# Low parts of the weights on VectorE, and mean and running-sum products queued with a margin, in a float32 encoder layer on one core

## The chip, the cores and the metric

The kernel runs on one core of one Trainium2 chip. The metric is the device time of one execution in microseconds (us). The kernel before has three timed runs: 1586.59, 1587.16 and 1590.54 us, median 1587.16. Engines are named as in the profile: PE is TensorE's matrix products, PEld its weight loads, DVE is VectorE, ACT is ScalarE, POOL is GpSimd, SP is SyncE, on which this kernel issues all its DMAs.

## The reference

One layer of a streaming encoder is computed for 1056 tokens: 1024 of a new stream and 32 that continue a running stream with 512 cached keys and values. There are 1024 features, 8 heads of 64, 512 channels in the convolution branch and 4096 hidden units, all in float32. Cut to what matters:

```python
p = einsum('btd,de->bte', x, w_in)        # GLU a, b | q | k | v | forget logits | 2 x 1024 gates
u = a * sigmoid(b)                         # convolution branch
y = depthwise_conv(u, w_dw) + b_dw         # causal, width 31
y_conv = silu(layer_norm(y)) @ w_conv_out  # mean and variance over the 512 channels
logf = log_sigmoid(p_f + b_f); c = cumsum(logf)
s = q k / 8 + c_q - c_k                    # masked, softmax, times v -> o
m = sigmoid(g_conv) * y_conv + sigmoid(g_attn) * (o @ w_attn_out)
x1 = layer_norm(alpha * x + m @ w_o)
x2 = layer_norm(alpha * x1 + relu(x1 @ w_up)**2 @ w_down)
```

Outputs are x2 and the new convolution rows, keys, values and log forget values.

## The kernel before, in words

**Layout and number format.** Features lie on the 128 partitions and tokens along the free axis, in three chunks of 352. A float32 product is made as three products of a faster format: each operand is split into a high part and a low part, and high x high, high x low and low x high are added in PSUM. So every weight is split on the chip. It arrives by DMA in halves of 128x512 (`raw`), ACT copies the half into `whi` with rounding, and a subtraction `raw - whi` leaves `wlo`. `Weights.split` does this for 264 halves; the first two subtractions are on DVE, 262 on POOL.

**Stages.** (1) Projections: GLU tiles, values, queries and keys (four tiles each, `ps_q`, `ps_k`), and gate tiles 0 to 5 (`ps_g`). (2) Attention over 8 heads and the cached stream (`ps_s` are its scores), with gate tiles 6 to 15 as filler products. (3) The merge, `w_o` with the first layer norm (`_n` in the names), eight blocks of hidden units (`ps_up`, `ps_dn`), and a tail with the last layer norm.

**The convolution branch.** Beside stage 1 a generator `conv()` issues the depthwise convolution on DVE: four channel tiles `ca`, 30 multiply-adds each of 128x1086. Then come three column blocks c0, c1, c2 of 362 columns, one after the other. Each is a layer norm over the channels: `total` adds the four tiles to `lns_dve_m`; `norm_rows` multiplies it on PE with a constant matrix (`ps_mu_c`), subtracts the mean on DVE, squares on ACT, adds the squares to `lns_dve_vc`, multiplies again (`ps_var_c`) and takes root and reciprocal (`rstd_c`). Then `done` makes, tile by tile, a multiply-add on DVE, a sigmoid on ACT (`csig`), a second multiply-add on DVE, the high part on ACT (`csh`) and the low part (`csl`), and DMAs both parts to a scratch `s_s`. A second generator, `forget()`, makes the log forget values `logf` in a chain of small DVE operations and sums them over the tokens with two products (`ps_cum`) and a transpose (`ps_cumt`) on PE.

**What sets the order.** Every engine works in the order of issue. The class `Issue` keeps a model clock for each engine. A generator yields what its next step needs; `service`, called between groups of products, goes on with a generator when `due(need)`, the modelled time at which these operands stand ready, is not past the modelled time of PE. What is left of the generators when the gate tiles of stage 1 are through is issued by `I.flush()` whatever its due time, and only then do the loads of the first head and the attention follow. In the listings and the profile, L202 and L206 are the product and the transpose in `Issue`, L214 an ACT operation, L218, L223, L227, L231 and L235 copy, tensor_tensor, tensor_scalar, scalar_tensor_tensor and reciprocal, L197 a DMA. In the changed kernel each of these stands three lines lower.

Of the kernel before, what the change touches and what calls it, by code (L numbers as in the profile page):

```python
# [17 lines left out]
P = 128  # L18
# [37 lines left out]
WARM = 19  # L56
GB = 2
# [21 lines left out]
class Issue:  # L79
    """Issues instructions and keeps a rough clock for each engine. Every engine works in the order of  # L80
    issue, so work that stands ready is put in front of work that would wait: `fill` and `service`."""
# [32 lines left out]
    def due(self, need):  # L114
        if callable(need):
            return 0.0 if need() else 1e12
        if isinstance(need[0], str):
            return max(self.t[e] for e in need[:-1]) - need[-1]
        return max(max(self.ready(a), self.free.get(a.tensor.name, 0.0)) for a in need)
# [19 lines left out]
    def finish(self, last):  # L139
        """issues what is left of a background stream and of those before it in its group"""  # L140
# [11 lines left out]
    def drain(self):  # L152
        """issues all background streams: the oldest that can go on, or else the first that can"""
# [6 lines left out]
    def pick(self, n, bias=0.0):  # L160
        """the engine that would be through with a tensor_tensor first"""
        pool, dve = (max(self.t[e], self.t["pe"] - 500) for e in ("pool", "dve"))
        return "pool" if pool + n * 1.97 + 150 + bias < dve + n * 1.01 + 80 else "dve"
# [74 lines left out]
class Slots:  # L238
    """A tile pool whose slots the clock knows"""
# [24 lines left out]
def hybrid_layer(ctx: ExitStack, tc, io):  # L264
# [15 lines left out]
    # ---- scratch in DRAM  # L280
# [20 lines left out]
    # ---- weights: streamed, split in two float32r parts that add up to the float32 exactly  # L301
# [10 lines left out]
    class Weights:  # L312
        def __init__(self):
            self.raw, self.parts, self.taken, self.done, self.halves = [], [], 0, 0, 0

# [7 lines left out]
        def split(self):  # L323
# [8 lines left out]
            tt(lo, raw, f32(hi), SUB, "dve" if i < 2 else "pool")  # L332
# [26 lines left out]
    def mm3(ps, terms, late=False, low=False):  # L359
        """ps = sum of w.T x over terms; each float32 product as hi hi + hi lo + lo hi"""  # L360
# [17 lines left out]
    # ---- layer norm of one block of tokens, features on the partitions of several tiles: 1/std and  # L378
    # the centred rows in place; a background stream whose steps come when their operands stand ready
# [16 lines left out]
    def norm_rows(pl, psl, tiles, mean, tag, n, s, engs, done):  # L396
        yield [s]
# [9 lines left out]
        yield [s]  # L407
# [7 lines left out]
    # sixteen rows of tiles: the inputs, then what the merge reads, then the residual and hidden units  # L415
# [11 lines left out]
    def gates(tiles, banks, staging, tag, bufs, xh_read=None):  # L427
        """the gates before their sigmoid; xh_read is called with the last tile's products of xh through"""
# [27 lines left out]
    # =============================================================== projections, convolution  # L456
    with pool("conv") as pv_, pool("a") as pa, pool("pa", space=PSUM) as psa:
# [40 lines left out]
        # products of ones, read by nobody, bring the tensor engine to its full clock as the inputs arrive  # L498
# [61 lines left out]
        def conv():  # L560
# [7 lines left out]
            for c in range(3):  # L568
                cs = slice(c * CC, (c + 1) * CC)
                tiles = [ca[j][:, cs] for j in range(NJ)]  # L570
                s = total(pv_, tiles, f"m{c}", CC, ("dve", "dve", "pool", "pool"))

                def done(rstd, c=c, cs=cs, tiles=tiles):
                    for j, y in enumerate(tiles):
# [8 lines left out]
                        tt(lo[:, j, :], y, f32(hi[:, j, :]), SUB, "pool")  # L583
                    for dst, src in ((s_s[0], hi), (s_s[1], lo)):
# [3 lines left out]
                        else:  # L588
# [5 lines left out]
                                     ("dve", "dve", "pool", "pool"), done)  # L594

        # ---- log sigmoid of the forget logits and its running sums
        logf = pa.tile([P, 9, H], F32, name="logf")

        def forget():
# [21 lines left out]
            yield [logf, lfs]  # L621
# [10 lines left out]
            yield [cum]  # L632
# [8 lines left out]
        # the first tiles go chunk by chunk, as the inputs arrive  # L641
# [17 lines left out]
        # ---- values, tokens on partitions  # L659
        for half in range(2):  # L660
            ws = [W.take() for g in range(2)]
            for t in range(9):
# [15 lines left out]
                tt(vs[:r, :, DH:P], vv, f32(vs[:r, :, 0:DH]), SUB, "pool")  # L678
# [12 lines left out]
        # ---- queries (times -1/8) and keys, features on partitions  # L691
        for m in range(4):
            for name in "qk":
                w = W.take()
                for c in range(NCH):
# [7 lines left out]
                    tt(lo, a, f32(hi), SUB, "pool")  # L703
# [23 lines left out]
    # =============================================================== attention, branch gates  # L727
    with pool("b") as pb, pool("pb", space=PSUM) as psb:
# [21 lines left out]
        # the first products of the merge, as the rows of the inputs come free  # L750
# [28 lines left out]
        # operands of one head: [kh; kh] on [qh; ql] and [kl; c, 1] on [qh; 1, -c] add up to all of  # L779
        # -(q k / 8 + c_q - c_k)  # L780
# [17 lines left out]
        # two heads of the running stream: their cached keys and values are split on the chip  # L798
# [87 lines left out]
        class Rows:  # L886
            """128 query rows of one head against their keys"""
# [56 lines left out]
        class Stream:  # L944
            """the new queries of two heads of the running stream against cached and new keys"""
# [93 lines left out]
    # =============================================================== merge, output projection, FFN  # L1039
# [62 lines left out]
    def run_sum(cs, m, s, tag, eng="dve"):  # L1102
        """adds tile m of a block of tokens to the running sum over features"""
# [12 lines left out]
    def squares(sq, t, total, nth, n, tag):  # L1116
        """squares one more tile and adds the square before it to the running sum"""
# [15 lines left out]
    def norm_out(cs, tag, s, emit, need=()):  # L1133
        """layer norm of a block of tokens in place, a background stream as well"""
# [66 lines left out]
    with pool("h") as ph:  # L1201
# [28 lines left out]
        def down_first(wd, cs):  # L1230
            """the first tiles, with what the newest hidden units add put last"""
# [44 lines left out]
        def output(cs, new=False):  # L1276
            """where a block of tokens puts its results: in place, or two tiles at a time"""
# [21 lines left out]
        # the last tokens go through the last hidden units block by block, with the weights kept  # L1299
# [28 lines left out]
        # the last block: the mean over its first tile is taken off as soon as it is known, which leaves  # L1328
# [134 lines left out]
```

## Time and profile before

| what | before |
|---|---|
| median of three runs | 1587.16 us |
| profiled execution, first to last instruction | 1585.9 us |
| PE busy | 1506.2 us (95%), 9524 products |
| DVE busy | 911.8 us (57%), 1385 instructions |
| ACT busy | 487.4 us (31%), 1048 instructions |
| POOL busy | 655.2 us (41%), 557 instructions |
| mean granted TensorE clock | 0.979 |

The profile is of one execution, and its own time is the span of 1585.9 us; the lowest timed run is 0.7 us above it and the median 1.3 us. A share of busy time is a mean over all stages; which wait ends last is read stage by stage. In rows of the timeline the first two numbers are the start and the duration of one instruction in us; `x4` says that four alike stand in the row; brackets give the idle time of the engine before it and what released it. Rows of windows give for a stretch its length, the busy time and the instructions of PE, PEld, DVE, ACT and POOL in that order, the granted TensorE clock, the DMA share and GB/s.

### The profile page before, as it was taken

The page shows a single profiled execution, that of the slowest core. Times are in us where ns is not written, and L with a number is a line of the kernel's source. Part 1 is how long each engine was busy: PE and PEld are TensorE (multiplying, and loading weights), DVE is VectorE, ACT ScalarE, POOL GpSimd, SP SyncE. Part 2 cuts the span into 40 slices and gives each one's busy share as a digit, 9 for nine tenths or more (in the row PEclk, how much of TensorE's full clock was granted, in tenths as well). Part 3 has the DMA queues.
Part 4 walks back from the last instruction along what each step waited for, and adds up shares of the span by engine and source line. Part 5 has one row for each costly group of instructions (what it writes and reads, how often), then busy time and mean ns, then how long its engine had stood idle before and what let it go on. Part 6 is the DMA issues. An engine that isn't in the chain of part 4 may idle for free.

```text
span 1585.9 us, 24681 instructions
## 1 busy us (share of the span) xinstructions
PE 1506.2 (95%) x9524; PEld 1476.5 (93%) x9524; DVE 911.8 (57%) x1385; ACT 487.4 (31%) x1048; POOL 655.2 (41%) x557
## 2 busy tenths in 40 slices
PE   9999598699999999999899999999999999999985
PEld 8999598698989999899899999999999999999984
DVE  4799999653656654864887243333424333342588
ACT  4211211453656655433554121111111111111133
POOL 2436576633445533657765222222222222222346
PEclk9999699899999999999999999999999999999998
DMA  6214443437555557626531111111111111114412
GB/s 199 69 46 137 134 136 125 151 114 219 152 142 147 146 150 269 210 87 190 154 96 54 47 47 41 54 41 50 44 47 47 41 54 41 54 41 140 153 37 73
DMA packets 113731, 165.56 MB, mean 104 GB/s; under 512 B 19146, under 2 KB 71626, under 8 KB 113614
## 3 DMA queue, kind: packets, MB, share of 16 engines
q1 hardware_dynamic: 113614, 163.99, 33.6%
q8 instruction: 75, 1.23, 0.3%
q14 instruction: 42, 0.34, 0.1%
HBM read 120.38 MB, written 43.54 MB: 103 GB/s over the span
## 4 chain that ended last, share of the span: by engine, by line
PE 67%; DVE 7%; issue 2%; ACT 1%; DMA 1%; POOL 1%; SPq 0%; DVEq 0%; ACTq 0%; POOLq 0%
PE ps_dn L202 22%; PE ps_up L202 22%; PE ps_g L202 8%; PE ps_yc L202 3%; PE ps_o L202 2%; PE ps_s L202 2%; PE ps_pv L202 2%; PE ps_tr L206 2%; PE ps_yo L202 2%; DVE acc L231 2%; DVE lnvar_n L223 2%; DVE acc L223 0%; DVE yg L223 0%; DVE rstd_n L235 0%; DMA g_s<-gt 0%
## 5 line engine op out<-in xcount | busy, mean ns | idle before, releaser
L223 POOL TENSOR_TENSOR wlo<-raw,whi 128x512 fp32r<-128x512 f32 (+1 forms) x262 | 381.8, 1478 | 605.6 <-ACT whi L214 598.7
L214 ACT ACTIVATE whi<-raw 128x512 fp32r<-128x512 f32 (+1 forms) x264 | 151.9, 623 | 396.9 <-issue 337.6
L202 PE MATMUL ps_dn<-hh,whi 128*128 128x352 f32 x768 | 249.3, 325 | 0.0
L202 PE MATMUL ps_dn<-hl,whi 128*128 128x352 f32 x768 | 247.8, 323 | 0.8 <-DVE hl L223 0.8
L202 PE MATMUL ps_dn<-hh,wlo 128*128 128x352 f32 x768 | 248.0, 323 | 0.0
L223 DVE TENSOR_TENSOR acc<-ps_dn,acc 128x352 f32<-128x352 f32 x168 | 87.8, 523 | 194.5 <-PE ps_dn L202 194.5
L231 DVE SCALAR_TENSOR_TENSOR ca<-u,prm,ca 128x1086 f32<-128x1086 f32 x120 | 197.7, 1648 | 2.5
L223 DVE TENSOR_TENSOR r<-r 128x352 f32<-128x352 f32 x96 | 52.5, 547 | 184.7 <-ACT r L214 184.7
L202 PEld LDWEIGHTS ps_dn<-hl,whi 128*128 128x128 f32 x768 | 144.5, 188 | 1.3 <-DVE hl L223 1.0
L202 PEld LDWEIGHTS ps_dn<-hh,whi 128*128 128x128 f32 x768 | 144.3, 188 | 0.5 <-DVE acc L223 0.2
L202 PEld LDWEIGHTS ps_dn<-hh,wlo 128*128 128x128 f32 x768 | 144.4, 188 | 0.0
L202 PE MATMUL ps_g<-xh,whi 128*128 128x352 f32 x384 | 132.4, 345 | 0.7 <-ACT gt L214 0.6
L214 ACT ACTIVATE r<-ps_up 128x352 f32<-128x352 f32 x96 | 44.5, 463 | 259.8 <-PE ps_up L202 253.6
L202 PE MATMUL ps_g<-xh,wlo 128*128 128x352 f32 x384 | 124.1, 323 | 0.0
L202 PE MATMUL ps_g<-xl,whi 128*128 128x352 f32 x384 | 121.9, 323 | 0.0
L223 DVE TENSOR_TENSOR hl<-r,hh 128x352 fp32r<-128x352 f32 x96 | 84.0, 875 | 3.3
L223 DVE TENSOR_TENSOR tl<-ps_tr,th 128x512 fp32r<-128x512 f32 (+2 forms) x96 | 51.2, 553 | 57.9 <-ACT th L214 56.0
L202 PE MATMUL ps_up<-x_0h,whi 128*128 128x352 f32 x256 | 82.9, 324 | 0.0
L202 PE MATMUL ps_up<-x_1h,wlo 128*128 128x352 f32 x256 | 82.4, 322 | 0.0
L202 PE MATMUL ps_up<-x_0h,wlo 128*128 128x352 f32 x256 | 82.4, 322 | 0.0
L202 PE MATMUL ps_up<-x_1h,whi 128*128 128x352 f32 x256 | 82.4, 322 | 0.0
L202 PE MATMUL ps_up<-x_0l,whi 128*128 128x352 f32 x256 | 82.3, 322 | 0.0
(283 smaller groups left out, 3834.6 us busy)
## 6 DMA issues: line engine op xcount, KB each, us to landing
raw<-in_w_in_dram SPq DMA_DIRECT2D x64, 256.0 KB
raw<-in_w_up_dram SPq DMA_DIRECT2D x64, 256.0 KB
raw<-in_w_down_dram SPq DMA_DIRECT2D x64, 256.0 KB
raw<-in_w_o_dram SPq DMA_DIRECT2D x48, 256.0 KB
g_s<-gt SPq DMA_DIRECT2D x48, 176.0 KB
yg<-g_s SPq DMA_DIRECT2D x48, 176.0 KB
xr<-in_x_dram SPq DMA_DIRECT2D x12, 352.0 KB
xr<-in_x_dram SPq DMA_DIRECT2D x24, 176.0 KB
```

Of the source, the lines that this page charges most:

```text
L202: self.nc.tensor.matmul(ps, lhsT=w, rhs=x, start=start, stop=stop)
L206: self.nc.tensor.transpose(ps, x, ident)
L214: self.nc.scalar.activation(out, in_, func, **kw)
L223: (self.nc.vector if eng == "dve" else self.nc.gpsimd).tensor_tensor(out, a, b, op)
L231: self.nc.vector.scalar_tensor_tensor(out, a, s, b, op0, op1)
```

## The change

1. `Weights.split` makes all 264 low parts on DVE (`self.engine`), where 262 were on POOL.
2. The low parts of values, queries and keys and of the convolution's output (`vs`, `ql`, `kl`, `csl`) go from POOL to DVE, and so do the additions of the convolution's layer norm: three on DVE in a row, where before one on DVE and one on POOL were joined by another on DVE.
3. `due` takes a pair of a float and a need, and adds the float to the due time. `ps_mu_c`, `ps_var_c`, `ps_cum` and `ps_cumt` are yielded with `MARGIN = 3000.0`, in the model's nanoseconds.

The rest of the diff takes out comments.

```diff
+MARGIN = 3000.0
...
     def due(self, need):
         if callable(need):
             return 0.0 if need() else 1e12
+        if isinstance(need[0], float):
+            return self.due(need[1]) + need[0]
...
+            self.engine = "dve"
...
-            tt(lo, raw, f32(hi), SUB, "dve" if i < 2 else "pool")
+            tt(lo, raw, f32(hi), SUB, self.engine)
...
     def norm_rows(pl, psl, tiles, mean, tag, n, s, engs, done):
-        yield [s]
+        yield (MARGIN, [s])
         mu = psl(f"mu_{tag}")[:, :n]
...
         s = total(pl, sq, f"v{tag}", n, engs)
-        yield [s]
+        yield (MARGIN, [s])
         var = psl(f"var_{tag}")[:, :n]
...
-                s = total(pv_, tiles, f"m{c}", CC, ("dve", "dve", "pool", "pool"))
+                s = total(pv_, tiles, f"m{c}", CC, ("dve",) * 4)
...
-                        tt(lo[:, j, :], y, f32(hi[:, j, :]), SUB, "pool")
+                        tt(lo[:, j, :], y, f32(hi[:, j, :]), SUB)
...
                 yield from norm_rows(pv_, bank, tiles, mean_c, f"c{c}", CC, s,
-                                     ("dve", "dve", "pool", "pool"), done)
+                                     ("dve",) * 4, done)
...
-            yield [logf, lfs]
+            yield (MARGIN, [logf, lfs])
...
-            yield [cum]
+            yield (MARGIN, [cum])
...
-                tt(vs[:r, :, DH:P], vv, f32(vs[:r, :, 0:DH]), SUB, "pool")
+                tt(vs[:r, :, DH:P], vv, f32(vs[:r, :, 0:DH]), SUB)
...
-                    tt(lo, a, f32(hi), SUB, "pool")
+                    tt(lo, a, f32(hi), SUB)
```

The change moves instructions in three places of interest. On PE, at the end of stage 1, the order before has the six mean and variance products of the convolution among the 432 products of gate tiles 0 to 5. After the first mean product come 30 gate products, then its variance product, then 102, and so on. The last gate product of stage 1 is the one of `ps_g5_2` shown here; 125 gate products stand between the variance product of c2 and it. Before the first scores (`ps_s_0_0`) come 90 filler products of gate tile 6.

```order
L202 MATMUL ps_mu_c0_72_2742<-lns_dve_m0_2687,mean_c_193 128x362
...
L202 MATMUL ps_var_c0_74_2795<-lns_dve_vc0_2756,mean_c_193 128x362
...
L202 MATMUL ps_mu_c1_79_2974<-lns_dve_m1_2910,mean_c_193 128x362
...
L202 MATMUL ps_var_c1_82_3028<-lns_dve_vc1_2988,mean_c_193 128x362
...
L202 MATMUL ps_mu_c2_87_3194<-lns_dve_m2_3139,mean_c_193 128x362
...
L202 MATMUL ps_var_c2_89_3257<-lns_dve_vc2_3208,mean_c_193 128x362
...
L202 MATMUL ps_g5_2_94_3423<-xh7_101,wlo25_2965 128x352
L202 MATMUL ps_g6_0_3499<-xh0_94,whi26_3096 128x352
...
L202 MATMUL ps_s_0_0_3498<-k1_0_3486,q1_0_3487 128x128
```

In the change, the first mean product stands after 366 of the 432 gate products and its variance product 54 further on, 12 before the last gate product. The other four stand behind the last gate product with nothing between them. Then 102 filler products lead to the first scores.

```order
L205 MATMUL ps_mu_c0_87_3205<-lns_dve_m0_3128,mean_c_193 128x362
...
L205 MATMUL ps_var_c0_90_3285<-lns_dve_vc0_3219,mean_c_193 128x362
...
L205 MATMUL ps_g5_2_89_3272<-xh7_101,wlo25_2886 128x352
L205 MATMUL ps_mu_c1_91_3347<-lns_dve_m1_3343,mean_c_193 128x362
L205 MATMUL ps_var_c1_92_3365<-lns_dve_vc1_3361,mean_c_193 128x362
L205 MATMUL ps_mu_c2_93_3402<-lns_dve_m2_3398,mean_c_193 128x362
L205 MATMUL ps_var_c2_94_3420<-lns_dve_vc2_3416,mean_c_193 128x362
L205 MATMUL ps_g6_0_3493<-xh0_94,whi26_2986 128x352
...
L205 MATMUL ps_s_0_0_3492<-k1_0_3480,q1_0_3481 128x128
```

So four products that had gate products between them now follow each other. In the same way the two `ps_cum` products stand after 42 products of the next key or query chunk, where they stood after 12, and `ps_cumt` 46 rows after the first of them, where it stood 28 after.

On DVE, the change's order for the last tiles of block c2 has the two multiply-adds of a tile, then its low part, and only then the next tile.

```order
L238 RECIPROCAL rstd_c2_3422<-rstd_c2_3422 128x362
L234 SCALAR_TENSOR_TENSOR ca0_205<-ca0_205,prm_86,rstd_c2_3422 128x362
L234 SCALAR_TENSOR_TENSOR ca0_205<-ca0_205,prm_86,csig2_0_3426 128x362
L226 TENSOR_TENSOR csl2_3430<-ca0_205,csh2_3429 128x362
L234 SCALAR_TENSOR_TENSOR ca1_206<-ca1_206,prm_86,rstd_c2_3422 128x362
L234 SCALAR_TENSOR_TENSOR ca1_206<-ca1_206,prm_86,csig2_1_3434 128x362
L226 TENSOR_TENSOR csl2_3430<-ca1_206,csh2_3429 128x362
L234 SCALAR_TENSOR_TENSOR ca2_207<-ca2_207,prm_86,rstd_c2_3422 128x362
```

Before, the low parts were POOL's and the next tile's multiply-add followed the second one of its predecessor directly.

On SP, before, the DMAs of block c2 were followed by the three of gate tile 5 and two weight halves, and then by the loads of the first head (`k1_0`, `q2_0` and so on). In the change, the gate tile's DMAs and the weight halves come ahead, and the loads of the first head stand directly behind the DMAs of all three blocks:

```order
L200 DMA raw63_3313<-in_w_in_dram 128x512
L200 DMA s0_s_73<-csh0_3319 128x4x362
L200 DMA s1_s_74<-csl0_3320 128x4x362
L200 DMA s0_s_73<-csh1_3374 128x4x362
L200 DMA s1_s_74<-csl1_3375 128x4x362
L200 DMA s0_s_73<-csh2_3429 128x4x300
L200 DMA s0_s_73<-csh2_3429 128x4x32
L200 DMA s1_s_74<-csl2_3430 128x4x300
L200 DMA s1_s_74<-csl2_3430 128x4x32
L200 DMA k1_0_3480<-kh_s_67 64x1024
L200 DMA q2_0_3466<-k2_0_3464 2x1024
```

In all, DVE has 1699 instructions in the change where it had 1385, and POOL 243 where it had 557.

In the first layer norm of stage 3 the generators are the same, but the model clocks are not: from a block's mean product to its variance product it was 60 products in each of the three blocks before, and is 90, 102 and 90 in the change. The variance product of the last block stood after 72 of the 288 products `ps_up` of the first hidden block, and now stands after 108; the products of that block's tokens begin at 192 in both.

## The prediction

> **What bounds the kernel now.** The page comes first: PE is busy for nearly the whole span, so time can only be won or lost where PE waits or runs at a lower clock.
>
> ```profile
> PE 1506.2 (95%) x9524; PEld 1476.5 (93%) x9524; DVE 911.8 (57%) x1385; ACT 487.4 (31%) x1048; POOL 655.2 (41%) x557
> PEclk9999699899999999999999999999999999999998
> ```
>
> Then the list of waits, which names what PE waits for:
>
> ```profile
> PE ps_mu_c L202 <- DVE lns_dve_m L223: 19.6, 2, 18.4
> PE ps_cum L202 <- DVE lfs L218: 19.4, 1, 19.4
> PE ps_var_n L202 <- DVE lnvar_n L223: 11.9, 5, 5.4
> PE ps_s L202 <- DMA q<-qh_s: 1.9, 1, 1.9
> ```
>
> Two long waits, for the log forget chain and for the convolution's first mean, make 38 us; the third line is the layer norms of stage 3. Last, the table of stretches shows where nothing is to be had: in attention (382 to 604) and in the hidden blocks (861 to 1510) PE is busy almost without a gap.
>
> ```profile
> 382.30:604.00 221.70, 219.72 (x1529) 206.62 (x1529) 138.85 (x303) 135.32 (x339) 102.41 (x137) 1.00 0.57 157
> 861.00:1510.00 649.00, 649.00 (x4048) 649.00 (x4047) 236.25 (x426) 100.12 (x195) 159.41 (x115) 1.00 0.19 59
> ```
>
> **Removed: the waits of stage 1.** The timeline of PE and the two stretches behind the long waits:
>
> ```profile
> 186.50 0.66 PE L202 MATMUL ps_cum<-logf,cst 128*128 128x64 f32 x2 [19.43 <-DVE lfs L218]
> 290.02 1.54 PE L202 MATMUL ps_mu_c<-lns_dve_m,mean_c 128*128 128x362 f32 x2 [18.40 <-DVE lns_dve_m L223]
> 337.94 0.88 PE L202 MATMUL ps_mu_c<-lns_dve_m,mean_c 128*128 128x362 f32 x2 [1.15 <-DVE lns_dve_m L223]
> 344.10 0.85 PE L202 MATMUL ps_var_c<-lns_dve_vc,mean_c 128*128 128x362 f32 x2 [0.49 <-DVE lns_dve_vc L223]
> 186.50:193.90 7.40, 7.40 (x27) 7.40 (x28) 6.82 (x20) 0.46 (x1) 6.43 (x4) 0.50 0.40 130
> 290.00:293.00 3.00, 2.98 (x8) 2.47 (x9) 1.52 (x5) 0.83 (x2) 2.80 (x3) 0.52 0.34 123
> ```
>
> 19.43 + 18.40 + 1.15 + 0.49 = 39.5 us of idle, and behind each long wait the clock is near half: 7.40 us at 0.50 lose 3.7, 3.0 us at 0.52 lose 1.4. Together 44.6 us. They do go: DVE is what is late, and it gets faster. Two of its multiply-adds beside POOL's subtractions take 8.05 us, one without takes 1.34:
>
> ```profile
> 141.34 8.05 DVE L231 SCALAR_TENSOR_TENSOR ca<-u,prm,ca 128x1086 f32<-128x1086 f32 x2
> 143.24 5.01 POOL L223 TENSOR_TENSOR wlo<-raw,whi 128x512 fp32r<-128x512 f32 x4
> 194.65 1.34 DVE L231 SCALAR_TENSOR_TENSOR ca<-u,prm,ca 128x1086 f32<-128x1086 f32 x1
> 4.66 0.69 DVE L223 TENSOR_TENSOR wlo<-raw,whi 128x512 fp32r<-128x512 f32 x1 [3.54 <-ACT whi L214]
> L231 DVE SCALAR_TENSOR_TENSOR ca<-u,prm,ca 128x1086 f32<-128x1086 f32 x120 | 197.7, 1648 | 2.5
> 48.40:290.00 241.60, 203.79 (x1365) 203.23 (x1364) 235.88 (x216) 44.67 (x109) 142.71 (x78) 0.92 0.36 114
> L223 POOL TENSOR_TENSOR wlo<-raw,whi x36: 1250/2100/2377, 48.9 to 280.1; 128x512 fp32r<-128x512 f32 x28, 128x520 fp32r<-128x520 f32 x8
>   ACT whi L214: 30.3, 6
> ```
>
> From 48.4 to 290 us DVE was busy 235.9 of 241.6. At 1.34 the 120 steps cost 161 us instead of 197.7, which frees 37. Added are 36 weight halves at 0.69 (25 us) and 42 small parts of values, queries and keys at about 0.5 (21 us): 245 us. But PE now reaches the first mean product only after 366 gate products instead of 12, near 305 (worked out below), 257 us after 48.4, so DVE is some 12 us early; for `ps_cum`, by the same sum over its shorter stretch, I estimate 7. The margin itself costs PE nothing, which has gate and key products until then. If DVE took POOL's six waits for `whi`, 30.3 us, 18 of them would come back as a stall; I take none, since a half is issued when the model has it ready.
>
> **Added: the convolution's end in front of the attention.** By the listings four of the six mean and variance products stand behind the last gate product with nothing between them, and the first head's loads behind all that. PE then waits for a chain DVE, ACT, DVE that before ran under gate products. Its steps, from blocks c2 and c0 of before:
>
> ```profile
> 338.85 1.86 DVE L223 TENSOR_TENSOR ca<-ca,ps_mu_c 128x362 f32<-128x362 f32 x4 [0.97 <-PE ps_mu_c L202]
> 345.58 2.42 DVE L235 RECIPROCAL rstd_c<-rstd_c 128x362 f32<-128x362 f32 x1 [1.63 <-ACT rstd_c L214]
> 348.03 0.60 DVE L231 SCALAR_TENSOR_TENSOR ca<-ca,prm,rstd_c 128x362 f32<-128x362 f32 x1
> 350.63 0.60 DVE L231 SCALAR_TENSOR_TENSOR ca<-ca,prm,csig 128x362 f32<-128x362 f32 x1 [2.00 <-ACT csig L214]
> 351.31 0.51 ACT L214 ACTIVATE csh<-ca 128x362 fp32r<-128x362 f32 x1 [0.71 <-issue]
> 351.90 0.97 POOL L223 TENSOR_TENSOR csl<-ca,csh 128x362 fp32r<-128x362 f32 x1 [6.83 <-ACT csh L214]
> 303.10 0.60 ACT L214 ACTIVATE csig<-ca,prm 128x362 f32<-128x362 f32 x1
> 310.50 0.53 DVE L223 TENSOR_TENSOR lns_dve_m<-ca,ca 128x362 f32<-128x362 f32 x1
> ```
>
> Variance product to reciprocal's end: 344.10 to 348.00, 3.9 us. First tile: 348.03 to 351.90, and 0.53 for the low part on DVE: 4.4. Each further tile, its low part in DVE's order ahead of the next tile: 0.63 + 0.63 (multiply-add, sigmoid, with hand-offs), 0.68 (350.63 to 351.31), 0.59 (to 351.90), 0.53: 3.06, three of them 9.2. Three additions of 0.53: 1.6. Mean product to variance product: 0.91 (337.94 to 338.85), 1.86, three additions, 0.2 of hand-off: 4.6.
>
> Let g be the end of the last gate product. `ps_var_c` of c0 starts 2.3 us ahead of it (12 products of 0.16, which is 649 us over 4048, and itself). Then 3.9, two weight halves that stand on DVE ahead of the tiles (1.4), 13.6 for the tiles, 1.6: the mean of c1 at g + 18.2, its variance at + 22.8, the mean of c2 19.1 later at + 41.9, its variance at + 46.5, the last low part done at + 64.0. From there to the scores rows of before give the parts, with the first gate product and the stretch that ends with the last one of stage 1:
>
> ```profile
> 269.53 0.32 PE L202 MATMUL ps_g<-xh,whi 128*128 128x352 f32 x1
> 290.00:365.10 75.10, 73.27 (x432) 70.51 (x432) 38.60 (x52) 39.19 (x72) 33.41 (x30) 0.98 0.41 138
> 359.61 0.82 POOL L223 TENSOR_TENSOR csl<-ca,csh 128x362 fp32r<-128x362 f32 x1
> 361.14 2.00 SPq L197 DMA_DIRECT2D s_s<-csl  x2
> 369.21 0.53 SPq L197 DMA_DIRECT2D k<-kh_s  x1
> 382.30 0.30 PE L202 MATMUL ps_s<-k,q 128*128 128x128 f32 x1 [1.91 <-DMA q<-qh_s]
> ```
>
> Low part to the end of the scratch's issue 2.7 (360.43 to 363.14), head loads to scores 13.1: g + 79.8. The four products run at half clock after so long a wait: 291.60 - 290.02 = 1.58 instead of 0.91, 2.7 in all: g + 82.5. Before, the last gate product ended at 365.1 and the scores began at 382.30, 17.2. Of the difference, 2.0 are 12 more filler products, which are saved later, and 2.4 the four products that are no longer ahead of g (0.6 each, my estimate below the 0.85 of their rows, whose ends are modelled). Added: 82.5 - 17.2 - 2.0 - 2.4 = 60.9. The net of stage 1 is 60.9 - 44.6 = **+16.3 us**. A check by another way: the chain from c0's mean to the last low part was 290.0 to 360.4 before; the mean's product now comes when PE has done 366 gate products of 0.16 from about 246.4 (269.5 less the 19.4 and 3.7), at 305, so 15 us later, with a chain that is no shorter.
>
> Bounds: a tile need not cost 3.06. The low parts of c2 on POOL were 2.57 apart (351.90 to 359.61 for four); with that, additions of 0.45 and full clock it is 8 us less, +8. Above, the half clock could last over filler products too: 3.7 more, as behind `ps_cum`.
>
> The Trainium skill (TensorE: Matmul & The Clock Gate, What's actually happening) says the clock halves after an idle window of some 3.4 us and is back after as long a busy one. By that rule each recovery would lose 1.7 us where the rows above lose 3.7 and 1.4, and the sum would be 1.7 us higher.
>
> **Moved: the first layer norm of stage 3.** Its waits and the slow stretch behind the longest:
>
> ```profile
> PE ps_var_n L202 <- DVE lnvar_n L223: 7.8, 3, 5.4
> 782.00:795.00 13.00, 7.61 (x33) 6.83 (x32) 9.89 (x13) 5.61 (x11) 8.62 (x7) 0.74 0.55 165
> ```
>
> The variance products move from 60 to 90, 102 and 90 products behind the means, 5 us or more, as much as the longest wait. 7.8 us go, and about 2.3 of half clock; 1 us may come back where the last block's hidden products follow its variance sooner. **-9.1**, at best -10, at worst 0.
>
> **Moved: 262 weight halves.** In the hidden blocks DVE is busy 236 of 649 us; 115 halves at 0.69 make 79 more, which PE's products hide: 0. In the tail no half is left: 0. In attention and merge DVE takes the softmax steps in one queue with low parts that wait for ACT; I take +1, at best 0, at worst the third rival's 13.
>
> Sum: 16.3 - 9.1 + 1 = **+8.2**. The span goes from 1585.9 to 1594.1, and the median, 1.3 above the span before, from 1587.16 to 1595.4, say **1595 us**.
>
> **The rivals.** *First, no change:* the hand-offs of the tail are short. Stage 1 then costs +8 by the bound above, the layer norm gains 10, attention nothing: 1585. For it: the 2.57. Against: DVE's order puts each low part ahead of the next tile, which POOL's did not.
>
> *Second, faster:* VectorE's relief goes on through attention and merge. All PE idle time there that isn't counted yet is 2.0 us in attention (221.70 less 219.72), and I estimate as much again and half in the merge; with the first rival's numbers +8 - 10 - 5 = -7, 1580. For it: the 8.05 beside the 1.34. Against: PE's gaps there are too small to give more. It decides if DVE operations there get shorter by more than the moved halves add. The Trainium skill (SBUF — State Buffer, Who interferes with whom) calls the port pair of the two engines an exclusive lock; the 8.05 agrees.
>
> *Third, slower still:* low parts block the softmax. POOL's waits for `whi` would become DVE's:
>
> ```profile
> L223 POOL TENSOR_TENSOR wlo<-raw,whi x20: 1276/1285/1741, 384.7 to 601.7; 128x512 fp32r<-128x512 f32 x20
>   ACT whi L214: 30.6, 7
> ```
>
> Seven waits of 4.4 us in attention; if three hold up a softmax step that PE waits for, 13 us in place of the 1: 1607. Against: the halves are issued when the model has them ready.
>
> That the change doesn't do what it says is excluded by the listings.
>
> **How the numbers follow.** Forecast 0.62, first rival 0.18, second 0.10, third 0.10. A measurement here tells 0.3%, 4.8 us, from no change: 1582.4 to 1591.9. The forecast's own range is 1589 to 1602; a tenth of it lies in the same band. So faster 0.10, the same 0.18 + 0.06 = 0.24, slower 0.56 + 0.10 = 0.66. The range takes in the first rival and the upper bounds: 1584 to 1604.
>
> **What would show it.** Right: the waits of `ps_cum` and of the first `ps_mu_c` are gone; two waits of `ps_mu_c` near 18 us and two of `ps_var_c` near 4 stand between 318 and 366, with DVE's sums as releaser; the scores begin near 400; `ps_var_n` waits only in the tail; 128x1086 steps take 1.3 us. Wrong: no idle time in front of the scores, a new wait of `ps_s` or `ps_pv` for DVE in attention, or gaps in the hidden blocks.

## The result and the profile after

The change is slower: 1606.53 us median (1604.71 to 1609.45, four runs) against 1587.16 us (1586.59 to 1590.54, four runs), a ratio of 1.0118 with the interval 1.0102 to 1.0133. On a second chip it was 1606.70 against 1590.09, 1.0107 (1.0092 to 1.0122). The forecast was 1595 with the range 1584 to 1604: the right side and less than half of the size, with the measured time above the range. The profiled execution has a span of 1602.9 us, 17.0 more than before.

The page after, part one and the clock of its second part:

```profile
PE 1507.9 (94%) x9524; PEld 1475.4 (92%) x9524; DVE 989.9 (62%) x1699; ACT 488.2 (30%) x1048; POOL 190.4 (12%) x243
PEclk9999999957999999999999999999999999999998
```

The two slow slices of the clock (at 186 and 290 us) are gone, and there is one deep dip in slices 9 and 10, from 320 to 400 us. The list of PE's waits has the same story:

```profile
PE ps_mu_c L205 <- DVE lns_dve_m L226: 33.6, 2, 17.9
PE ps_g L205 <- ACT gt L217: 13.2, 2, 9.8
PE ps_var_c L205 <- DVE lns_dve_vc L226: 7.4, 2, 3.7
PE ps_var_n L205 <- DVE lnvar_n L226: 6.4, 4, 3.8
PE ps_pv L205 <- DVE tl L226: 3.1, 3, 2.4
PE ps_tr L209 <- DVE tl L226: 3.0, 1, 3.0
```

`ps_cum` is no longer there. `ps_mu_c` waits twice, not for the first block but for the second and third, and `ps_g` (0.6 us before) and `ps_pv` are new. The timeline of PE, with the two stretches of the stage's end (columns as in the prediction):

```profile
171.95 0.33 PE L205 MATMUL ps_cum<-logf,cst 128*128 128x64 f32 x2
305.14 0.47 PE L205 MATMUL ps_mu_c<-lns_dve_m,mean_c 128*128 128x362 f32 x1
316.77 0.32 PE L205 MATMUL ps_g<-xh,wlo 128*128 128x352 f32 x1
332.84 1.54 PE L205 MATMUL ps_mu_c<-lns_dve_m,mean_c 128*128 128x362 f32 x2 [15.75 <-DVE lns_dve_m L226]
338.06 1.58 PE L205 MATMUL ps_var_c<-lns_dve_vc,mean_c 128*128 128x362 f32 x2 [3.68 <-DVE lns_dve_vc L226]
357.50 1.54 PE L205 MATMUL ps_mu_c<-lns_dve_m,mean_c 128*128 128x362 f32 x2 [17.87 <-DVE lns_dve_m L226]
362.73 1.57 PE L205 MATMUL ps_var_c<-lns_dve_vc,mean_c 128*128 128x362 f32 x2 [3.68 <-DVE lns_dve_vc L226]
398.45 0.33 PE L205 MATMUL ps_s<-k,q 128*128 128x128 f32 x2
317.10:364.96 47.86, 6.24 (x9) 2.01 (x9) 27.83 (x49) 20.23 (x33) 0.00 (x0) 0.53 0.22 77
364.96:403.00 38.04, 24.87 (x123) 24.04 (x124) 13.28 (x21) 10.88 (x21) 0.38 (x1) 0.78 0.51 146
```

PE comes to the end of its gate products at 317.1, 48 us ahead of the kernel before, and then does 9 instructions in 47.9 us: two for each of the four mean and variance products, and the end of the last gate product. Its waits for the convolution's sums there are 33.6 + 7.4 = 41.0 us. The 13.2 us of `ps_g` lie behind them, among the filler products in front of the scores.

Cut at four first products (the softmax transposes, the merge, `w_o`, the first hidden block), the two executions differ as follows.

| stretch | before | after | difference |
|---|---|---|---|
| to the first transpose | 386.6 | 403.0 | +16.4 |
| attention | 213.4 | 219.0 | +5.6 |
| merge up to `w_o` | 108.6 | 108.8 | +0.2 |
| `w_o` and first layer norm | 103.5 | 98.6 | -4.9 |
| hidden blocks and tail | 773.8 | 773.5 | -0.3 |

Six filler products more (1 us) stand ahead of the first transpose in the change than before, so that much of the +16.4 is work that attention has less of.

### The profile page after: what moved, and what is told of

Same layout as the page of the kernel before. It is cut to its first block, busy times and chain, and to the rows that moved or that the text cites. A ratio compares the mean times of both kernels' runs of the same rounds, so it can differ in the third digit from the quotient of the medians.

```text
span 1602.9 us, 24659 instructions
## 1 busy us (share of the span) xinstructions
PE 1507.9 (94%) x9524; PEld 1475.4 (92%) x9524; DVE 989.9 (62%) x1699; ACT 488.2 (30%) x1048; POOL 190.4 (12%) x243
## 4 chain that ended last, share of the span: by engine, by line
PE 80%; DVE 11%; ACT 3%; issue 2%; DMA 2%; SPq 1%; POOL 0%; DVEq 0%; ACTq 0%; POOLq 0%
PE ps_dn L205 22%; PE ps_up L205 20%; PE ps_g L205 10%; PE ps_v L205 3%; PE ps_glub L205 3%; PE ps_k L205 3%; PE ps_glua L205 3%; PE ps_q L205 3%; PE ps_yc L205 2%; PE ps_pv L205 2%; PE ps_s L205 2%; PE ps_o L205 2%; PE ps_tr L209 2%; PE ps_yo L205 2%; DVE acc L234 1%
## 5 line engine op out<-in xcount | busy, mean ns | idle before, releaser
L226 DVE TENSOR_TENSOR wlo<-raw,whi 128x512 fp32r<-128x512 f32 (+1 forms) x264 | 175.1, 704 | 113.1 <-ACT whi L217 109.9
L234 DVE SCALAR_TENSOR_TENSOR ca<-u,prm,ca 128x1086 f32<-128x1086 f32 x120 | 161.8, 1349 | 2.4
L205 PE MATMUL ps_g<-xh,whi 128*128 128x352 f32 x384 | 132.7, 346 | 13.8 <-ACT gt L217 13.2
L226 POOL TENSOR_TENSOR acc<-acc,lnmu_n 128x352 f32<-128x352 f32 x10 | 10.8, 1109 | 663.1 <-ACT lnmu_n L217 663.1
L205 PEld LDWEIGHTS ps_g<-xh,whi 128*128 128x128 f32 x384 | 74.6, 194 | 15.7 <-ACT gt L217 13.7
L205 PE MATMUL ps_up<-x_0h,wlo 128*128 128x352 f32 x256 | 82.5, 322 | 0.0
L205 PE MATMUL ps_up<-x_1h,wlo 128*128 128x352 f32 x256 | 82.5, 322 | 0.0
```

Of the source, the lines that this page charges most:

```text
L205: self.nc.tensor.matmul(ps, lhsT=w, rhs=x, start=start, stop=stop)
L226: (self.nc.vector if eng == "dve" else self.nc.gpsimd).tensor_tensor(out, a, b, op)
L234: self.nc.vector.scalar_tensor_tensor(out, a, s, b, op0, op1)
```

## The experiments

Each ratio is to the kernel before on the same chip.

### Is it the margin or VectorE's load? (two runs)

**Margin zero**

```diff
-MARGIN = 3000.0
+MARGIN = 0.0
```

> The changed kernel with MARGIN = 0.0, so all moves to VectorE stay and nothing is queued later on purpose. Theory D (VectorE's own load puts the convolution's chain late, the margin hardly matters): the order still has four of the six mean and variance products behind the last gate product; the first mean product stands 18 products earlier (2.9 us), at about 302.2, where VectorE has its sums at 300.9; scores near 395.5, time 1603 to 1605 against 1606.5 of the change. Rival M (the margin makes the chain late): the four products find their operands ready, PE waits less than 10 us in front of the scores, time at or below 1590.

Measured: 1602.25 us, ratio 1.0069 (1.0052 to 1.0086). The first mean product is at 301.86, the scores 5.3 us ahead of the change's (393.1), the four late products are still late. The margin is about a third of the change's delay in front of the scores, not the whole. This bore out theory D, with a little more from the margin than it had.

**Margin only**

```diff
+        if isinstance(need[0], float):
+            return self.due(need[1]) + need[0]
...
-        yield [s]
+        yield (MARGIN, [s])
```

(and the same for the running sums; every low part where it was).

> The kernel before with the margin alone; every low part on the engine it had. Theory D: VectorE has the sums of the first block at 290 as before; the first mean product stands 24 products later (3.9 us), so its wait falls from 18.4 to about 14.5, that of ps_cum from 19.4 to about 16.5; the chain still ends near 360 and only the last variance product stands behind the gate products; scores near 376 to 384, time 1582 to 1589. Rival M: the margin alone brings most of the 19 us, 1598 or more, with waits of 15 us for ps_mu_c behind the last gate product.

Measured: 1598.03 us, ratio 1.0052 (1.0037 to 1.0067): slower, which theory D had not expected. The list of waits, then VectorE's and PE's rows of the second block:

```profile
PE ps_mu_c L205 <- DVE lns_dve_m L226: 19.4, 1, 19.4
PE ps_cum L205 <- DVE lfs L221: 16.8, 1, 16.8
319.20 0.54 DVE L226 TENSOR_TENSOR lns_dve_m<-lns_dve_m,lns_pool_m 128x362 f32<-128x362 f32 x1 [1.65 <-POOL lns_pool_m L226]
323.79 0.47 PE L205 MATMUL ps_mu_c<-lns_dve_m,mean_c 128*128 128x362 f32 x1
```

The waits the margin was put there for stay, since VectorE is late by far more than 3 us; and where operands do stand ready (319.7), the product comes 4 us later, in a chain of six such products. The last variance product falls to 360.2 (before 344.1), the first transpose to 396.4. So rival M had a part in it: the margin lengthens the chain, and the chain is what the scores wait for. On this chip the margin alone costs 7.0 us and the moves alone (margin zero) 11.2; together they cost 16.6 and 19.4 on the two chips above.

### Which of the moves? (two runs)

**Low parts of weights on POOL from the attention on**

```diff
         I.flush()
+        W.engine = "pool"
```

> The changed kernel, but from the end of the projection stage on the low parts of the weights are POOL's again. Theory F (in attention VectorE's queue with low parts costs PE 5.5 us, in the first layer norm their absence on POOL brings some 4 us): stage 1 as in the change, scores near 398; from the first transposes to the merge the lag against the kernel before stays at 16 us instead of growing to 22; the waits of ps_var_n come back (7.8 us); time 1602 to 1606. Rival: attention's growing lag is filler order and clock, not VectorE; then it stays near 22 and the time is 1607 or more.

Measured: 1603.22 us, ratio 1.0081 (1.0066 to 1.0096). The rows of stretches, attention and then `w_o` with the layer norm, of before, of the change and of this kernel:

```profile
386.60:600.00 213.40, 211.53 (x1476) 199.08 (x1476) 135.51 (x295) 129.16 (x322) 97.13 (x133) 1.00 0.56 153
708.60:812.10 103.50, 97.27 (x585) 95.49 (x585) 72.16 (x95) 53.82 (x99) 81.83 (x61) 0.97 0.51 154
```

```profile
403.00:622.00 219.00, 211.13 (x1467) 197.50 (x1466) 147.08 (x309) 128.36 (x322) 74.81 (x114) 1.00 0.54 152
730.80:829.40 98.60, 95.17 (x586) 93.70 (x585) 79.76 (x131) 47.79 (x87) 18.95 (x19) 1.00 0.52 167
```

```profile
402.20:615.60 213.40, 211.55 (x1477) 199.16 (x1477) 135.19 (x295) 129.14 (x322) 96.51 (x132) 1.00 0.55 153
724.20:828.40 104.20, 97.90 (x585) 96.07 (x585) 73.03 (x95) 53.81 (x99) 81.70 (x61) 0.97 0.51 153
```

Attention is 213.4 us long again to a tenth, and the layer norm's gain is gone. Theory F is shown for attention: it is the engine of the low parts that costs 5.6 us there. A line of VectorE's waits in that stretch of the change, and two rows of its timeline:

```profile
DVE wlo L226 <- ACT whi L217: 9.9, 7, 2.2
```

```profile
616.53 1.29 DVE L226 TENSOR_TENSOR wlo<-raw,whi 128x512 fp32r<-128x512 f32 x2 [1.65 <-ACT whi L217]
617.93 1.28 DVE L226 TENSOR_TENSOR tl<-ps_tr,th 128x512 fp32r<-128x512 f32 x2
```

VectorE stands 1.65 us for ACT's `whi`, works 1.3 us on low parts, and the softmax's `tl`, for which PE waits 2.4 us in `ps_pv`, comes behind. PE's longest wait of the stretch, 3.0 us in `ps_tr`, ends behind VectorE's copies of the cached keys and values (568.4 to 571.7); how the low parts lead to that one is not shown.

**All low parts of weights on POOL, the rest as changed**

```diff
-            tt(lo, raw, f32(hi), SUB, self.engine)
+            tt(lo, raw, f32(hi), SUB, "dve" if i < 2 else "pool")
```

> The changed kernel, but all low parts of weights except the first two on POOL as before; the small low parts, the convolution's sums and the margin stay as changed. Theory D: POOL has 66 of its 143 us between 48 and 290 left, so VectorE's steps are held up about half as much (mean near 1.5 us), its 42 small parts add 21 us, and the sums of the first block are ready near 291; the model places the product at 276, so PE waits about 15 us there, and the scores begin near 384; time 1585 to 1592. Rival M: mean products late behind the gate products again, time 1600 or more.

Measured: 1602.90 us, ratio 1.0077 (1.0062 to 1.0092), a miss by more than 10 us. The multiply-adds were as foreseen (1516 ns), the first block's sums came at 296 instead of 291, and `ps_mu_c` waited 9.7 us for them; but with the margin the third block fell behind the last gate product with a wait of 12.4, and the scores to 396.7. The expectation had left out what the margin does to the chain.

### Would other work cover the chain? (three runs and the change again)

```diff
-GA = 6
+GA = 10
```

**The change with ten gate tiles in stage 1**

> The changed kernel with GA = 10: gate tiles 6 to 9 (288 products, 46 us of PE) are done in front of the attention's loads instead of as filler in it; nothing else. Theory C (the scores begin when the convolution's chain on VectorE has ended, some 16 us after it; PE's long waits in stage 1 only filled the time until then, and more gate products can fill it instead): the order has gate products between the mean and variance products, the waits of ps_mu_c fall from 33.6 us to below 6, the scores begin near 402 with 46 us more work done, 26 us ahead of the kernel before; attention with less filler gives some of it back, time 1562 to 1580. Rival: PE's time is set by something else in front of the scores (loads, memory given back), so that the 40 us of waits only move: 1598 or more.

**The kernel before with ten**

> The kernel before with GA = 10 and nothing else: the control for the run above. Its stalls of 19.4 and 18.4 us stay, since they stand ahead of the gate products, and its end of stage 1 had work already; theory C says no gain, and the run shows what the attention loses with less filler: 1585 to 1600. If it gains as much as the change does with GA = 10, the gain there is not the chain's cover.

**Margin zero, POOL from the attention on, and ten**

> The changed kernel with MARGIN = 0.0, GA = 10, and the low parts of the weights on POOL from the attention on. Theory C: the chain is 5 us shorter without the margin, but gate products cover it anyway, the last variance product comes with 72 gate products still to go; no wait of ps_mu_c over 4 us, scores near 397; attention without VectorE's extra load 5 us better, the first layer norm 5 us worse; time 1555 to 1575, ahead of both kernels. Rival: as above, 1595 or more.

**The change itself on the same chip**

> The changed kernel once more, on the same chip as the three others, so that they can be set against it: 1.010 to 1.0135 of the kernel before, by its earlier runs.

Measured: 1612.06, 1637.34, 1605.88 and 1606.70 us, ratios 1.014 (1.0124 to 1.0155), 1.030 (1.0283 to 1.0317), 1.0095 (1.008 to 1.011) and 1.0107. The times are off in the three, for one reason: with four filler tiles less in attention the kernel loses 47 us, which the control shows and I had put at 13 at most. Against the control theory C holds: with ten gate tiles the change is 25 us faster than the kernel before, where 26 were worked out, and its first transposes come at 410.1 instead of 431.6. The first fence has waits of the change with ten, the second of the kernel before with ten:

```profile
PE ps_mu_c L205 <- DVE lns_dve_m L226: 0.2, 1, 0.2
PE ps_tr L209 <- ACT ob L217: 20.0, 16, 9.5
```

```profile
PE ps_mu_c L202 <- DVE lns_dve_m L223: 20.1, 2, 18.8
PE ps_cum L202 <- DVE lfs L218: 19.4, 1, 19.4
PE ps_tr L206 <- ACT ob L214: 20.0, 15, 9.0
```

So what the change took from PE's stalls is real work time, if something stands there to do. With six gate tiles nothing does.

### Shorten the chain (four runs)

**Copies on ACT, in the kernel before** (the high parts of values, queries and keys)

```diff
-                cp(vs[:r, :, 0:DH], vv)
+                act(vs[:r, :, 0:DH], vv, AF.Copy)
...
-                    cp(hi, a)
+                    act(hi, a, AF.Copy)
```

> The kernel before with one edit: the high parts of values, queries and keys (42 copies, some 12 us) are made on ACT instead of VectorE. Theory D + C (the time at which VectorE has the first block's sums, 290 us, sets the scores, by PE's products behind it and by the chain of about 92 us): the sums are ready near 278, ps_cum's wait falls by some 6 us, the scores begin near 370 to 373, time 10 to 12 us under the kernel before, ratio 0.992 to 0.994. Rival (the engine does not matter, the waits of stage 1 are made by the order alone): the mean product is placed 42 products earlier, so its wait grows by 7 us and the time is the same within 3 us.

Measured: 1593.93 us, ratio 1.0023 (1.0013 to 1.0032). No gain: a miss. The sums of the first block came at 285 instead of 290 (278 was expected), `ps_cum` waited 23.9 us instead of 19.4. VectorE's multiply-adds of the convolution, before, here, and in the change:

```profile
L231 DVE SCALAR_TENSOR_TENSOR ca<-u,prm,ca 128x1086 f32<-128x1086 f32 x120 | 197.7, 1648 | 2.5
```

```profile
L231 DVE SCALAR_TENSOR_TENSOR ca<-u,prm,ca 128x1086 f32<-128x1086 f32 x120 | 209.9, 1749 | 3.9
```

```profile
L234 DVE SCALAR_TENSOR_TENSOR ca<-u,prm,ca 128x1086 f32<-128x1086 f32 x120 | 161.8, 1349 | 2.4
```

Without the copies the same 120 steps took 12 us more, beside the same number of POOL's subtractions. The 42 copies had been 21.7 us of VectorE's busy time, not some 12, and only 4.6 us of that came out at the first block's sums: much of what VectorE no longer spent on copies it spent on longer multiply-adds. A part of the miss is order. VectorE now had 74 of the 120 steps ahead of the log forget values where it had 69, so these came 6.7 us later, and PE's last gate product ended at 370.6 instead of 365.1.

**The tiles of a block staggered, in the change**

```diff
+                    for j in range(NJ + 2):
+                        yield ("dve", 1500)
+                        if j < NJ:
...
+                            stt(y, y, par("lcg", j), rstd, MUL, MUL)
...
+                        if 0 < j <= NJ:
...
+                            stt(y, y, par("lcb", j - 1), sg[j - 1], ADD, MUL)
+                            act(hi[:, j - 1, :], y, AF.Copy)
+                        if j > 1:
+                            tt(lo[:, j - 2, :], tiles[j - 2], f32(hi[:, j - 2, :]), SUB)
```

> The changed kernel with the tiles of a block staggered: first multiply-add of a tile, second of the tile before it, low part of the tile before that. Same instructions, MARGIN and engines. Theory C: a block's tiles take about 8 us instead of 11.6 on VectorE, three blocks shorten the chain by 10 to 11 us, the scores begin near 387, time 1594 to 1597, ratio 1.003 to 1.005. Rival (loads and memory given back set the scores): 1603 or more.

Measured: 1592.13 us, ratio 1.0013 (1.0003 to 1.0022), 14.6 us under the change (1606.70 on another chip). The first and last rows of a block's tiles, of the change and of this kernel:

```profile
367.39 0.60 DVE L234 SCALAR_TENSOR_TENSOR ca<-ca,prm,rstd_c 128x362 f32<-128x362 f32 x1
...
379.90 0.54 DVE L226 TENSOR_TENSOR csl<-ca,csh 128x362 fp32r<-128x362 f32 x1 [0.57 <-ACT csh L217]
```

```profile
355.96 1.10 DVE L234 SCALAR_TENSOR_TENSOR ca<-ca,prm,rstd_c 128x362 f32<-128x362 f32 x2
...
362.50 1.19 DVE L226 TENSOR_TENSOR csl<-ca,csh 128x362 fp32r<-128x362 f32 x2
```

13.1 us became 7.7 for the same twelve instructions, 5.4 a block where 3.6 were expected, and the scores begin at 382.9 instead of 398.5. The chain does set the scores.

**Both, in the kernel before**

> The kernel before with the copies on ACT and the staggered tiles. Theory: with the products placed as early as here PE, not the chain, sets the scores (552 gate and filler products of 0.16 behind the first mean product, 88 us, against a chain of some 82), so the stagger adds little: within 3 us of the copies alone, ratio 0.990 to 0.994. Rival: the chain still sets them, then 8 to 10 us less than the copies alone.

Measured: 1593.01 us, ratio 1.0018 (1.0006 to 1.003): as the copies alone, as expected for the stagger; the level was missed with the copies. In the kernel before the chain isn't what PE waits for in front of the scores, so a shorter one brings nothing. SyncE's rows show what is: its last store of the convolution and its first load of a head, in the kernel before with the copies on ACT, and in the change:

```profile
358.71 2.12 SPq L197 DMA_DIRECT2D s_s<-csl  x2
374.69 0.54 SPq L197 DMA_DIRECT2D k<-kh_s  x1
```

```profile
380.90 1.68 SPq L200 DMA_DIRECT2D s_s<-csl  x2
382.63 1.40 SPq L200 DMA_DIRECT2D k<-kh_s  x1
```

In the kernel before the loads begin 4.1 us behind the last gate product (365.1 to 369.2), and so they do here (370.6 to 374.7), 14 us behind the convolution's last store. In the change, in all runs built on it and in the kernel before with the margin, they begin within 0.1 us of that store. They read nothing that the convolution writes. They stand behind its stores in SyncE's order, and the change's trace also has POOL wait for `csl` before it clears one of attention's buffers (`sq`), which points to memory handed on. No run put the loads ahead of the stores, so which of the two holds them is open.

**All together, in the change** (margin zero, copies on ACT, staggered tiles, POOL from the attention on)

> The changed kernel with MARGIN = 0.0, copies on ACT, staggered tiles, and the low parts of weights on POOL from the attention on. Theory C + D: the sums of the first block are ready near 289, the chain is some 10 us shorter, scores near 363 to 368, attention and layer norm as before; time 14 to 19 us under the kernel before, ratio 0.988 to 0.991, ahead of both kernels. Rival: the scores stay behind 380 and the ratio at or above 0.998.

Measured: 1567.43 us, ratio 0.9855 (0.9841 to 0.987), faster than both kernels and by more than expected. The first transpose is at 366.0.

### What was still open (two runs)

**Copies on ACT, in the change**, the same edit as above:

> The changed kernel with the copies of values, queries and keys on ACT and nothing else: the edit that brought nothing in the kernel before. Theory L (beside POOL's subtractions VectorE's time is POOL's time as well, so what leaves VectorE is filled by longer multiply-adds; without POOL its own work counts): the 42 copies leave 14 us and more; the first mean product stands 120 products earlier, near 286, without a wait; the chain then meets PE at the last gate product, near 317, the four products follow it and the scores begin near 381 instead of 398; time 1588 to 1593, ratio 0.999 to 1.002. Rival (copies on ACT bring nothing in either kernel): 1603 or more, ratio 1.008 or more.

Measured: 1592.55 us, ratio 1.002 (1.0009 to 1.0031), 14 us under the change. The first block's sums came at 280.7 instead of 300.9, 20.2 us earlier, where the same edit beside POOL had made 4.6. The multiply-adds stay at 1348 ns. Theory L is borne out for VectorE's time. That the two kernels' times answer so differently has a second cause: only in the change does VectorE's chain set the scores.

**The mended change, with VectorE's low parts from the merge on**

```diff
         while I.step(True):
             pass
+        W.engine = "dve"
```

> The mended change (MARGIN = 0.0, copies on ACT, staggered tiles, low parts of weights on POOL in attention), but from the merge on VectorE makes the low parts again. If the first layer norm's gain of 5 us belongs to VectorE's low parts, with variance products after 90 and more products, it comes back here without attention's loss: 1561 to 1564, ratio 0.981 to 0.984, waits of ps_var_n and ps_mu_n together about 4 us. Rival (the 5 us are only what attention's lag gave back, a shift of filler): as the mended change, 0.985 to 0.987.

Measured: 1561.91 us, ratio 0.9824 (0.9808 to 0.9841), the best of all, 28 us under the kernel before. Its two stretches and the waits that are left in front of the scores:

```profile
364.80:578.50 213.70, 211.66 (x1476) 199.11 (x1475) 135.16 (x295) 129.17 (x322) 96.51 (x132) 1.00 0.56 153
687.20:785.80 98.60, 95.16 (x586) 93.66 (x586) 79.56 (x130) 47.63 (x87) 19.17 (x19) 1.00 0.55 167
```

```profile
PE ps_g L205 <- ACT gt L217: 9.6, 2, 6.0
PE ps_mu_c L205 <- DVE lns_dve_m L226: 7.1, 1, 7.1
PE ps_var_c L205 <- DVE lns_dve_vc L226: 3.7, 1, 3.7
```

98.6 us as in the change, 213.7 as before: loss and gain of the last two terms are apart. In the first layer norm `ps_var_n` waits 2.4 us and `ps_mu_n` 1.8, as expected. Whether the layer norm's gain comes from the engine or from the wider order that the model makes with it (90 products and more between mean and variance, against 60 with POOL) isn't told apart, since the one goes with the other here.

## Why the prediction was right in its way and wrong in its size

- **Removed, 44.6 us: right.** The three long and short stalls and both slow stretches are gone; the gate products end at 317.1, where 365.1 - 44.6 - 2.4 = 318.1 was worked out. VectorE's lead was smaller than said, but there: its sums end at 300.9, by the row below from its timeline, and the mean product starts at 305.14, so 4.2 us instead of 12; 6.5 instead of 7 for `ps_cum`. VectorE was busy 233.5 of the 252.5 us from 48.4 on. The sum had 245 us of work and no idle time: the work was put 11.5 us too high, and 19.0 us of VectorE's own waiting was left out.

```profile
299.79 1.11 DVE L226 TENSOR_TENSOR lns_dve_m<-lns_dve_m,ca 128x362 f32<-128x362 f32 x2
```

- **Added, the chain in front of the scores: right in the mechanism and the order of its steps, and in part lucky in its size.** From the last gate product: mean of c1 + 15.7 (said 18.2), its variance + 21.0 (22.8), mean of c2 + 40.4 (41.9), variance + 45.6 (46.5), last low part + 63.3 (64.0), scores + 81.4 (82.5). The four products took 1.54 to 1.58 us at half clock, as from the row of before. The sum adds their 2.7 us of half clock only at its end. With them in place the last low part was due at + 66.7 and came 3.4 us sooner, and from there to the scores it took 18.0 us instead of 15.8, so two errors nearly cancel. To the first transposes the difference is +16.4 us and the sum said +16.3, which had 2.0 us of filler saved later already taken off.
- **Third term, the first layer norm: mis-sized.** -9.1 was said, "at worst 0"; it measured -4.9. The longest wait went as said, but 1 us for what comes back was too small: PE's waits of this layer norm fell from 7.8 us to 4.7, with `ps_mu_n` as a new one. In its list from 720 to 870 us:

```profile
PE ps_var_n L205 <- DVE lnvar_n L226: 2.3, 2, 1.7
PE ps_mu_n L205 <- DVE lnsum_n L226: 1.8, 1, 1.8
```

  VectorE now makes `w_o`'s low parts in the same stretch (DVE 72.2 us of 103.5 became 79.8 of 98.6); that these cause the waits that came back is likely and not shown.
- **Fourth term, attention: mis-sized.** +1 was said, the trace has +5.6. It is the third rival's mechanism at less than half of its price: the trace of before had seven waits of POOL for `whi`, I left them all but out because "the halves are issued when the model has them ready", and VectorE stood in that queue: seven waits again, 9.9 us where POOL's were 30.6.
- **Hidden blocks and tail, 0: right** (-0.3).

So the step that failed is the price of the low parts behind stage 1: -9.1 + 1 = -8.1 us was forecast, -4.9 + 5.6 = +0.7 was measured. 4.6 and 4.2 us make the 8.8 by which the profiled span (+17.0) differs from the sum (+8.2). The timed median is 19.4 above the one before on the first chip, 16.6 on the second. On the first it lies 3.6 us above the profiled span, where the 1.3 of before had been taken over; that is another 2.3 us of the miss.

What the prediction did not see is how the margin and the moves share the main term. The moves free PE and put VectorE's chain 11 us later (290.0 to 300.9); the margin makes it 5 us longer. Of the rivals, the first fell with its price: the tiles cost 2.9 us each, not 2.57. The second's relief in attention did not appear.

On the clock: the first filler products behind the chain, in PE's timeline of the change:

```profile
365.41 0.49 PE L205 MATMUL ps_g<-xl,whi 128*128 128x352 f32 x1
...
368.05 0.33 PE L205 MATMUL ps_g<-xl,whi 128*128 128x352 f32 x1
```

The slow products end 3.1 us after the first of them at 364.96, near the 3.4 us that the Trainium skill (TensorE: Matmul & The Clock Gate, What's actually happening) gives; the 7.4 us at half clock behind the kernel before's `ps_cum` are not matched by it. Behind the next wait, of 9.8 us, the products are slow from 384.1 to 388.6, 4.5 us. PE waits for `gt` again behind both slow stretches, so neither shows in the time of the scores.

## What to carry to other kernels

A stall of the busiest engine is worth only what the chain behind it lets through: ask when the next stage's inputs are there, by whichever engine, before counting the stall as gain. Here 39.5 us of PE's idle time went away and 41 us came back in front of the scores, since the loads for the scores stand behind a chain of VectorE and ACT; shortening that chain (staggered tiles, copies on ACT, no margin) and leaving attention's low parts to POOL turned a loss of 1.1% into a gain of 1.8%. A margin that is to keep an engine from waiting also delays the links of a dependent chain, here by 5.3 us up to the scores.

## What the runs showed of the hardware that I had not expected

Work taken off VectorE does not come back in full while GpSimd has work beside it: beside POOL's subtractions, taking 42 copies (21.7 us) off VectorE brought its sums only 4.6 us forward, with the 120 multiply-adds going from 1648 to 1749 ns; the same edit with the subtractions on VectorE (14.2 us of copies, multiply-adds at 1349 and 1348 ns) brought them 20.2 us forward. That goes with the exclusive lock in the Trainium skill (SBUF — State Buffer, Who interferes with whom), which the prediction had used for the speed of one step, not for what an edit is worth. And pairs of matrix instructions 5 to 20 us apart did not bring the clock back: it was 0.53 in the 47.9 us of the chain.
